# Input projection: the products with the high part of a weight tile all ahead of those with its low part

## The chip, the cores and the metric

The program runs on one core of one Trainium2 chip. The metric is device time in microseconds (us) from the start of one execution to its end; lower is better. Each time shown here is a median of several executions, or the span of one execution that the hardware profiler recorded.

## The reference, cut to what matters

One layer of a hybrid decoder is computed for 256 prompt tokens and 8 x 4 sample tokens, 288 token rows in all:

```python
def hybrid_layer(x, ...):
    proj = x @ p['w_in']                  # (288 x 2048) @ (2048 x 5968): the input projection
    y_r, s_T, new_shift = rwkv_time_mix(proj[..., :RWKV_COLS], ...)     # 16 heads x 64, a recurrence
    y_n, ... = nsa_mix(proj[..., RWKV_COLS:], ...)    # compressed, selected and window attention
    h = jnp.concatenate([y_r, y_n], axis=-1) @ p['w_out']
    x = layer_norm(DEEPNORM_ALPHA * x + h, ...)
    f = peer_ffn(x, ...)                  # product-key experts: scores, top 16, gathered rows
    return layer_norm(DEEPNORM_ALPHA * x + f, ...)
```

The change touches the first line alone, and there only the order in which its partial products are summed.

## The kernel before

**The input projection.** The function `product` (L404) computes one block of up to 128 projected columns for all 288 tokens. The 2048 rows of the weight are taken as 16 chunks of 128, four to a weight tile, so a block has four weight tiles. A tile arrives by one or two transfers into `wraw` (4 buffers, L412). ScalarE casts it to the rounded high part `wh` (L415), and VectorE, or GpSimd for the last tile of a block, subtracts to get the low part `wl` (L417); `wh` and `wl` have 3 buffers each. The tokens are split in the same way, once, into `XH` and `XL`. TensorE then accumulates three products for each chunk in one of two PSUM banks `pj` (L422): `wh` by `XH`, `wh` by `XL`, `wl` by `XH`. That is 12 matmuls for a tile, 48 for a block, and 2256 for the 47 blocks of the kernel. The block is read out by `shift_mix` (L755, for the recurrence) or by a copy on ScalarE (L493, L507, for the attention).

**What else runs in that stage.** While the projection runs, GpSimd gathers pages of the compressed cache (`co`, 4 buffers, issued at L453 behind the last `wl` that GpSimd made), VectorE adds them up with weights (`CA`, L474 and L476), and VectorE, ScalarE and GpSimd do the elementwise work of the recurrence for each pair of heads (`head_pair`, L757 to L824). Later the chunked recurrence itself (`prompt_steps`, lines from L1085 on) is woven into the projection of the attention columns.

**What sets the order.** The kernel is written as generators that `weave` interleaves in program order, and then a list scheduler in the framework orders each engine's instructions by when it believes their operands to be ready. Each engine executes its own list strictly in that order. So an edit to the order of matmuls can also change what stands ahead of what on the other engines, and on the DMA queue of SyncE (SP), which issues the weight transfers.

**After the projection** come the sample states and the attention over the caches, the output projection with its own loop (L1706), the query products of the experts (L1865), a dense product of all experts (L1911), and the weighted sum of the expert rows (L1957 to L2119). None of them calls `product`.

Of the kernel before, what the change touches and what calls it, by code (L numbers as in the profile page):

```python
# [2 lines left out]

# [1 line left out]

# [143 lines left out]
def hybrid_decode_step(ctx: ExitStack, tc: tile.TileContext, a, outs, dbg=None):  # L149
# [37 lines left out]
    def bank(tag="pb"):  # L187
        places = [(pool, nm, n) for _, div in psum for t_, pool, nm, n in div for _ in range(n) if t_ == tag]
        turn[tag] = k = (turn.get(tag, -1) + 1) % len(places)
        pool, nm, n = places[k]  # L190
        return pool.tile([P, 512], F32, name=tag, tag=nm, bufs=n)
# [169 lines left out]
    for q in range(8):  # L361
        pb = bank(("p0", "p1")[q % 2])
        for t in range(2):
            for e in range(2):
                k = 2 * q + e
# [38 lines left out]
    def product(pool, pieces, xh, xl, zero=None, n=P, lo=None, m=8, nt=NT):  # L404

        pb = bank("pj")
        for o in range(0, 16, m):
            w = pool([P, m, P], "wraw", bufs=WB)
            if zero is not None:
                ve.memset(w[:, :, zero[0]:zero[1]], 0.0)  # L410
            for src, c0, c1 in pieces:
                last[0] = sy.dma_start(w[:, :, c0:c1], src.rearrange("(k p) c -> p k c", p=P)[:, o:o + m])  # L412
            wh = pool([P, m, P], "wh", F32R, bufs=WH)
            wl = pool([P, m, P], "wl", F32R, bufs=WH)
            sc.copy(wh[:, :, :n], w[:, :, :n])  # L415
            en = lo or (gp if o // m in LOG else ve)
            i_ = en.tensor_tensor(wl[:, :, :n], w[:, :, :n], wh[:, :, :n].bitcast(F32), OP.subtract)  # L417
            if en is gp:
                last[1] = i_
            for k in range(m):  # L420
                for wi, xi in ((wh, xh), (wh, xl), (wl, xh)):
                    last[2] = pe.matmul(pb[:n, :nt], wi[:, k, :n], xi[(o + k) // 8][:, (o + k) % 8, :nt],  # L422
                                        start=(o + k == 0 and wi is wh and xi is xh), stop=(o + k == 15 and wi is wl))
        return pb

    w_in = a["w_in"][0]
    def proj(*cols, **kw):
        o, pieces = 0, []
        for c0, c1, *at in cols:
            o = at[0] if at else o  # L430
            pieces.append((w_in[:, c0:c1], o, o + c1 - c0))
            o += c1 - c0
        return product(wp, pieces, *([x_[:, :8], x_[:, 8:]] for x_ in (XH0, XL0)), m=WM, **kw)
# [1332 lines left out]
    for t in range(2):  # L1766
        for q in range(4):
# [5 lines left out]
            for e in range(4):  # L1773
                k = 4 * q + e
# [430 lines left out]
```

## Time and profile before

| what | us |
|---|---|
| median of 3 executions | 2430.81 |
| lowest and highest of them | 2426.59, 2439.01 |
| the profiled execution, its own time | 2431.03 |
| its span in the trace | 2429.3 |
| first and last start of a matmul of the input projection (L422) | 20.1, 516.6 |
| busy time of those 2256 matmuls, by product: wh XH, wh XL, wl XH | 231.6, 227.7, 232.8 |
| TensorE idle just ahead of them, by product | 13.8, 0.0, 11.4 |
| casts to wh on ScalarE (188), mean of one | 0.616 |
| subtractions to wl on VectorE (141), mean of one | 0.716 |
| subtractions to wl on GpSimd (47), median of one | 1.293 |

The page gives the granted clock of TensorE as a share of full speed, a mean of 0.954 over the span. An instruction's idle time is that of its engine just before it, and the arrow names what ended it. Matmuls are pipelined: one shows as 0.29 us long, and the next starts 0.13 us after it.

### The profile page before, as it was taken

The page shows a single profiled execution, that of the slowest core. Times are in us where ns is not written, and L with a number is a line of the kernel's source. Part 1 is how long each engine was busy: PE and PEld are TensorE (multiplying, and loading weights), DVE is VectorE, ACT ScalarE, POOL GpSimd, SP SyncE. Part 2 cuts the span into 40 slices and gives each one's busy share as a digit, 9 for nine tenths or more (in the row PEclk, how much of TensorE's full clock was granted, in tenths as well). Part 3 has the DMA queues.
Part 4 walks back from the last instruction along what each step waited for, and adds up shares of the span by engine and source line. Part 5 has one row for each costly group of instructions (what it writes and reads, how often), then busy time and mean ns, then how long its engine had stood idle before and what let it go on. Part 6 is the DMA issues. An engine that isn't in the chain of part 4 may idle for free.

```text
span 2429.3 us, 42430 instructions
## 1 busy us (share of the span) xinstructions
PE 2241.3 (92%) x15564; PEld 1877.2 (77%) x15564; DVE 1755.8 (72%) x4053; ACT 824.8 (34%) x1609; POOL 1292.9 (53%) x1342
## 2 busy tenths in 40 slices
PE   7989999896897898889999999998998999999996
PEld 7978898894644566678888888887777888887885
DVE  5789766555374345789867777566777899998888
ACT  4433222223333343220111111112776444443443
POOL 5678423223264211648755556464442688876772
PEclk9989999998698898899999999998999999999998
DMA  7777985447468974989899999997664899999994
GB/s 219 233 227 237 277 226 166 128 135 240 159 232 257 330 261 160 347 303 382 306 376 372 373 388 385 357 405 273 188 193 122 312 359 361 359 361 356 349 361 178
DMA packets 311025, 683.42 MB, mean 281 GB/s; under 512 B 82239, under 2 KB 184577, under 8 KB 309889
## 3 DMA queue, kind: packets, MB, share of 16 engines
q1 hardware_dynamic: 229600, 341.93, 41.9%
q0 software_dynamic: 81216, 338.78, 38.9%
q8 instruction: 123, 2.02, 0.3%
q14 instruction: 86, 0.70, 0.1%
HBM read 665.04 MB, written 23.88 MB: 284 GB/s over the span
## 4 chain that ended last, share of the span: by engine, by line
PE 69%; DMA 8%; DVE 7%; issue 6%; POOL 5%; ACT 3%; SPq 1%; POOLq 0%; DVEq 0%; ACTq 0%
PE pb L2119 18%; PE ph L1911 15%; PE pj L422 7%; PE pj L1865 5%; PE pa L1706 3%; PE px L1957 3%; PE pa L1990 2%; DMA co<-in_cache_cmp_kv,gidx 2%; POOL rows L453 2%; DMA rows<-in_peer_u_g,gi 2%; PE p L1096 2%; PE pt L1949 2%; PE fs L2009 1%; PE sa L923 1%; PE ss L1535 1%
## 5 line engine op out<-in xcount | busy, mean ns | idle before, releaser
L1911 PE MATMUL ph<-Xfd,ur 128*128 128x256 f32 x2304 | 497.6, 379 | 0.0
L1911 PEld LDWEIGHTS ph<-Xfd,ur 128*128 128x128 f32 x2304 | 437.6, 190 | 59.4
L453 POOL DMA_INDIRECT rq<-in_peer_v_g,gi x256 | 380.6, 1487 | 150.4 <-DVE fP L2092 85.6
L453 POOL DMA_INDIRECT rows<-in_peer_u_g,gi x256 | 297.3, 1161 | 204.6 <-DVE rows L1835 117.1
L1835 DVE SCALAR_TENSOR_TENSOR rows<-rows,x1a 128x896 f32<-128x896 f32 x256 | 280.9, 1104 | 136.2 <-DMA rows<-in_peer_u_g,gi 133.6
L422 PE MATMUL pj<-XH,wh 128*128 128x288 f32 (+1 forms) x752 | 231.6, 308 | 13.8 <-DVE ss L755 6.0
L422 PE MATMUL pj<-XH,wl 128*128 128x288 f32 (+1 forms) x752 | 232.8, 310 | 11.4 <-POOL wl L417 5.8
L422 PE MATMUL pj<-XL,wh 128*128 128x288 f32 (+1 forms) x752 | 227.7, 303 | 0.0
L2092 DVE SCALAR_TENSOR_TENSOR fP<-rq,ge,fP 128x640 f32<-128x640 f32 x254 | 223.6, 880 | 2.5
L2119 PE MATMUL pb<-vl,ah 128*128 128x512 f32 (+1 forms) x768 | 207.1, 378 | 0.8
L2119 PE MATMUL pb<-vh,al 128*128 128x512 f32 (+1 forms) x768 | 205.4, 375 | 0.0
L2119 PE MATMUL pb<-vh,ah 128*128 128x512 f32 (+1 forms) x768 | 186.7, 378 | 13.4 <-ACT vh L2111 10.9
L1912 ACT COPY AW<-ph 128x256 f32<-128x256 f32 x128 | 76.5, 614 | 360.4 <-PE ph L1911 321.0
L415 ACT CAST wh<-wraw 128x512 fp32r<-128x512 f32 (+1 forms) x188 | 114.7, 616 | 228.9 <-PE pj L422 178.8
L2119 PEld LDWEIGHTS pb<-vh,ah 128*128 128x128 f32 x768 | 144.8, 195 | 35.7 <-ACT vh L2111 13.9
L476 DVE SCALAR_TENSOR_TENSOR CA<-co,wbc,CA 128x256 f32<-128x256 f32 x248 | 129.8, 561 | 46.7 <-DMA co<-in_cache_cmp_kv,gidx 46.6
L2119 PEld LDWEIGHTS pb<-vl,ah 128*128 128x128 f32 x768 | 145.0, 195 | 23.0 <-DVE vl L2112 3.8
L422 PEld LDWEIGHTS pj<-XH,wl 128*128 128x128 f32 (+1 forms) x752 | 145.5, 194 | 21.6 <-DVE wl L417 8.0
L422 PEld LDWEIGHTS pj<-XH,wh 128*128 128x128 f32 (+1 forms) x752 | 146.0, 194 | 20.1 <-DVE ss L755 6.4
L2119 PEld LDWEIGHTS pb<-vh,al 128*128 128x128 f32 x768 | 145.0, 194 | 19.4
L422 PEld LDWEIGHTS pj<-XL,wh 128*128 128x128 f32 (+1 forms) x752 | 146.0, 194 | 1.5 <-issue 1.2
L417 DVE TENSOR_TENSOR wl<-wraw,wh 128x512 fp32r<-128x512 f32 (+1 forms) x141 | 99.9, 716 | 41.2 <-ACT wh L415 38.3
(869 smaller groups left out, 4281.1 us busy)
## 6 DMA issues: line engine op xcount, KB each, us to landing
ur<-in_peer_u_t SPq DMA_DIRECT2D x128, 576.0 KB
wraw<-in_w_in SPq DMA_DIRECT2D x152, 256.0 KB
cw<-in_w_out SPq DMA_DIRECT2D x32, 512.0 KB
wraw<-in_w_out SPq DMA_DIRECT2D x32, 512.0 KB
wraw<-in_peer_wq SPq DMA_DIRECT2D x32, 512.0 KB
cw<-in_peer_wq SPq DMA_DIRECT2D x32, 512.0 KB
wraw<-in_w_in SPq DMA_DIRECT2D x64, 128.0 KB
co<-in_state_win_kv SPq DMA_DIRECT2D x16, 512.0 KB
```

Source lines behind the costliest of these rows:

```text
L415: sc.copy(wh[:, :, :n], w[:, :, :n])
L417: i_ = en.tensor_tensor(wl[:, :, :n], w[:, :, :n], wh[:, :, :n].bitcast(F32), OP.subtract)
L422: last[2] = pe.matmul(pb[:n, :nt], wi[:, k, :n], xi[(o + k) // 8][:, (o + k) % 8, :nt], start=(o + k == 0 and wi is wh and xi is xh), stop ...
L453: gp.indirect_dma_start(out=dst, out_offset=None, in_=rows_, in_offset=bass.IndirectOffsetOnAxis(ap=ix, axis=0))
L476: ve.scalar_tensor_tensor(d_, x_, w_, d_, op0=OP.mult, op1=OP.add)
L1706: pe.matmul(acc[t], xi[:, e, P * t:P * t + P], wi[:, e, :], start=(k == e == n_ == 0), stop=(k == 6 and e == 1 and n_ == 2))
L1835: i_ = ve.scalar_tensor_tensor(r_, r_, 1.0, X1a[t], op0=OP.mult, op1=OP.mult, accum_out=h_)
L1865: pe.matmul(pq[c][:, :NPR], w[:, k, 128 * c:128 * c + 128], XT[:, 4 * g + k, :], start=(g == k == 0), stop=(g == k == 3))
L1911: mm = pe.matmul(ph[:, :NPR], w[:, e, :], Xfd[:, e, :], start=(e == 0), stop=(e == NDB - 1))
L1912: return mm, sc.copy(AW[:, i1 // 64, :, i1 % 64], ph[:, :NPR])
L2092: ve.scalar_tensor_tensor(fP[t], r_, w_, fP[t], op0=OP.mult, op1=OP.add)
L2119: pe.matmul(acc[3 * t + q][:, :n_], wi[:, P * t:P * t + P], xi[:, 512 * q:512 * q + n_], start=(k == 0 and wi is ah and xi is vh), stop=(k ...
```

## The change

The three products of a chunk were issued chunk by chunk. Now a weight tile's eight products with `wh` are issued first, chunk by chunk, and then its four products with `wl`. The flags that start and end the accumulation stay with the first and the last matmul of the block. Nothing else is edited.

```diff
+import itertools
...
-            for k in range(m):
-                for wi, xi in ((wh, xh), (wh, xl), (wl, xh)):
+            for pairs in (((wh, xh), (wh, xl)), ((wl, xh),)):
+                for k, (wi, xi) in itertools.product(range(m), pairs):
                     last[2] = pe.matmul(pb[:n, :nt], wi[:, k, :n], xi[(o + k) // 8][:, (o + k) % 8, :nt],
                                         start=(o + k == 0 and wi is wh and xi is xh), stop=(o + k == 15 and wi is wl))
```

Two lines are added above, so a line of the changed kernel has a number that is higher by 2.

**TensorE.** Here is the border between the first two weight tiles of the first block (tile 306/307, then 326/327; 96 columns wide), before:

```order
L422 MATMUL pj_301<-XL_131,wh_306 96x288
L422 MATMUL pj_301<-XH_130,wl_307 96x288
L422 MATMUL pj_301<-XH_130,wh_326 96x288
L422 MATMUL pj_301<-XL_131,wh_326 96x288
L422 MATMUL pj_301<-XH_130,wl_327 96x288
```

and now:

```order
L424 MATMUL pj_301<-XL_131,wh_306 96x288
L424 MATMUL pj_301<-XH_130,wl_307 96x288 x4
L424 MATMUL pj_301<-XH_130,wh_326 96x288
L424 MATMUL pj_301<-XL_131,wh_326 96x288
L424 MATMUL pj_301<-XH_130,wh_326 96x288
```

The first matmul that reads `wl` was the third of its tile and is now the ninth; the last that reads `wh` was the eleventh and is now the eighth.

**VectorE.** The next place is in the work for the fifth pair of heads. `ss_2598<-pj_2512` (L755) is the last part of the readout of a block from its PSUM bank, `wl_2809` the low part of the first weight tile of a later block, `CA` the adds of gathered pages, the other rows the recurrence's elementwise work. Before:

```order
L821 TENSOR_TENSOR ss_2598<-kx_2644,Di_2636 128x32
L755 SCALAR_TENSOR_TENSOR ss_2598<-pj_2512,ommu_181,Tmu_2600 128x32
L476 SCALAR_TENSOR_TENSOR CA_1633<-co_2671,wbc_91,CA_1633 128x256 x2
L821 TENSOR_TENSOR st_2597<-ta_2620,Di_2636 128x128 x2
L821 TENSOR_TENSOR ss_2598<-ta_2620,Di_2636 128x32
L476 SCALAR_TENSOR_TENSOR CA_1633<-co_2671,wbc_91,CA_1633 128x256 x2
L809 TENSOR_TENSOR BV_95<-pb_2650,st_2597 128x128 x2
L809 TENSOR_TENSOR BV_95<-pb_2650,ss_2598 128x32
L476 SCALAR_TENSOR_TENSOR CA_1633<-co_2700,wbc_91,CA_1633 128x256 x2
L782 SCALAR_TENSOR_TENSOR L_2920<-CT1_100,tw_2912 128x256
L476 SCALAR_TENSOR_TENSOR CA_1633<-co_2700,wbc_91,CA_1633 128x256 x2
L417 TENSOR_TENSOR wl_2809<-wraw_2806,wh_2808 128x512
```

and now:

```order
L757 SCALAR_TENSOR_TENSOR st_2597<-pj_2512,ommu_181,Tmu_2600 128x128 x2
L818 TENSOR_TENSOR st_2597<-rx_2585,De_2633 128x2x64 x2
L803 SCALAR_TENSOR_TENSOR kk_2643<-K8_278,PT_63,pb_2641 128x288
L478 SCALAR_TENSOR_TENSOR CA_1633<-co_2671,wbc_91,CA_1633 128x256
L478 SCALAR_TENSOR_TENSOR CA_1633<-co_2700,wbc_91,CA_1633 128x256
L757 SCALAR_TENSOR_TENSOR ss_2598<-pj_2512,ommu_181,Tmu_2600 128x32
L820 TENSOR_TENSOR ss_2598<-rx_2585,ss_2598 128x32
L817 TENSOR_TENSOR st_2597<-kk_2643,De_2633 128x2x64 x2
L478 SCALAR_TENSOR_TENSOR CA_1633<-co_2700,wbc_91,CA_1633 128x256
L804 TENSOR_TENSOR kx_2644<-K8_278,fk_2624 128x288
L819 TENSOR_TENSOR ss_2598<-kk_2643,ss_2598 128x32
L419 TENSOR_TENSOR wl_2809<-wraw_2806,wh_2808 128x512
```

Behind the readout, `wl_2809` stood behind eight adds of pages and seven other instructions, and now stands behind one add and five others. In return two adds have come between the parts of the readout.

**The queue of SP**, at the start of the output projection. `cw` and `wraw` are tiles of weights of 512 KB each, for the sample tokens and for the prompt tokens. Before:

```order
L1568 DMA SKT<-in_subkeys_t 128x2048
L1695 DMA wraw<-in_w_out 128x2x512 x2
L1533 DMA cw<-in_w_out 128x1024
L1695 DMA wraw<-in_w_out 128x2x512
L1533 DMA cw<-in_w_out 128x1024 x2
```

and now:

```order
L1570 DMA SKT<-in_subkeys_t 128x2048
L1697 DMA wraw<-in_w_out 128x2x512 x3
L1535 DMA cw<-in_w_out 128x1024 x2
L1747 DMA wraw<-in_peer_wq 128x4x256 x2
L1535 DMA cw<-in_w_out 128x1024
```

The third tile of the prompt tokens has moved ahead of one tile of the sample tokens. From the dense product of the experts (L1911) on, the orders of TensorE and of SP are unchanged, while on the other engines a few instructions of the expert selection near its start changed places.

## The prediction

> **What bounds the kernel now.** I read the page's busy shares first, then its costliest groups.
>
> ```profile
> PE 2241.3 (92%) x15564; PEld 1877.2 (77%) x15564; DVE 1755.8 (72%) x4053; ACT 824.8 (34%) x1609; POOL 1292.9 (53%) x1342
> ...
> L422 PE MATMUL pj<-XH,wh 128*128 128x288 f32 (+1 forms) x752 | 231.6, 308 | 13.8 <-DVE ss L755 6.0
> L422 PE MATMUL pj<-XH,wl 128*128 128x288 f32 (+1 forms) x752 | 232.8, 310 | 11.4 <-POOL wl L417 5.8
> ```
>
> TensorE is busy 92% of the span, so only its idle time can come back. The edit touches one stage. There, TensorE is idle 13.8 us ahead of a product `wh` by `XH`, and 11.4 us ahead of a product `wl` by `XH`. The 11.4 us is what the edit aims at and is 0.47% of the span, so even all of it would hardly be seen. The view by stretches gives the stage and some parts of it. Its columns are length, busy time of PE, PEld, DVE, ACT and POOL with counts, clock, DMA share and GB/s:
>
> ```profile
> 20.00:517.00 497.00, 465.82 (x4981) 425.65 (x4980) 351.00 (x746) 162.18 (x338) 255.39 (x395) 0.96 0.71 206
> 130.00:153.00 23.00, 17.03 (x106) 14.55 (x105) 22.84 (x58) 7.56 (x17) 18.20 (x31) 0.87 0.79 235
> 165.00:174.00 9.00, 6.64 (x41) 5.62 (x42) 9.00 (x21) 2.88 (x8) 6.13 (x12) 1.00 0.61 172
> 174.00:190.00 16.00, 15.34 (x89) 13.24 (x87) 15.12 (x38) 5.83 (x13) 14.94 (x28) 0.89 0.70 218
> 190.00:217.00 27.00, 24.07 (x168) 19.69 (x167) 25.28 (x67) 10.56 (x25) 21.79 (x43) 0.97 0.92 285
> ```
>
> Over the stage VectorE is busy 351 of 497 us, but not evenly: between 165 and 217 it works 9.00 + 15.12 + 25.28 = 49.4 of 52 us. An engine that has 2.6 us of rest there can be late for TensorE whatever order TensorE takes.
>
> **What the edit gives a `wl`.** The timeline of TensorE shows the pace (start, length, instruction). Between these two rows lie 12 steps:
>
> ```profile
> 25.74 0.29 PE L422 MATMUL pj<-XL,wh 128*128 128x288 f32 x1
> ...
> 27.33 0.29 PE L422 MATMUL pj<-XL,wh 128*128 128x288 f32 x1
> ```
>
> (27.33 − 25.74) / 12 = 0.133 us from one matmul to the next. The first `wl` matmul was third of its tile and becomes ninth, so six matmuls of work that needs no `wl` come ahead of it: 6 × 0.133 = **0.80 us of slack for each weight tile**. The last read of `wh` was eleventh and becomes eighth, so its buffer is freed 3 × 0.133 = 0.40 us sooner; the cast that refills it, and the `wl` behind that, can start by as much earlier. The last reads of `wl` and of the block are where they were, so `wraw`, `wl` and `pj` come free as before. There are as many matmuls, weight loads, casts and transfers as before, and no instruction or wait is added.
>
> **Where the 11.4 us are.** I looked at every idle time ahead of a `wl` matmul in the timeline. There are 13, each behind exactly two matmuls of its tile. These nine matter by name, with two other waits that follow them:
>
> ```profile
> 40.16 0.40 PE L422 MATMUL pj<-XH,wl 128*128 128x288 f32 x1 [0.56 <-POOL wl L417]
> ...
> 45.23 0.58 PE L422 MATMUL pj<-XH,wh 128*128 128x288 f32 x1 [3.48 <-DVE lo L755]
> ...
> 126.33 0.40 PE L422 MATMUL pj<-XH,wl 128*128 128x288 f32 x1 [2.03 <-POOL wl L417]
> ...
> 129.44 0.61 PE L422 MATMUL pj<-XH,wl 128*128 128x288 f32 x1 [0.17 <-DVE wl L417]
> ...
> 152.42 0.61 PE L422 MATMUL pj<-XH,wh 128*128 128x288 f32 x1 [5.97 <-DVE ss L755]
> ...
> 165.28 0.40 PE L422 MATMUL pj<-XH,wl 128*128 128x288 f32 x1 [0.76 <-DVE wl L417]
> ...
> 173.56 0.40 PE L422 MATMUL pj<-XH,wl 128*128 128x288 f32 x1 [1.48 <-DVE wl L417]
> ...
> 188.70 0.40 PE L422 MATMUL pj<-XH,wl 128*128 128x288 f32 x1 [0.66 <-DVE wl L417]
> ...
> 205.66 0.40 PE L422 MATMUL pj<-XH,wl 128*128 128x288 f32 x1 [0.72 <-DVE wl L417]
> ...
> 209.53 0.40 PE L422 MATMUL pj<-XH,wl 128*128 128x288 f32 x1 [0.82 <-POOL wl L417]
> ...
> 215.37 0.54 PE L422 MATMUL pj<-XH,wl 128*128 128x288 f32 x1 [1.40 <-DVE wl L417]
> ```
>
> Behind 217 four are left, shown here as a group over 217 to 517:
>
> ```profile
> L422 PE MATMUL pj<-XH,wl 128*128 128x288 f32 x398 | 122.5, 308 | 2.8 <-POOL wl L417 2.4 <-DVE wl L417 0.4
> ```
>
> ```profile
> 421.89 0.40 PE L422 MATMUL pj<-XH,wl 128*128 128x288 f32 x1 [1.65 <-POOL wl L417]
> ```
>
> With 0.80 us of slack each wait loses the smaller of itself and 0.80. Part by part:
>
> *Up to 153: nothing.* What is won at 40.16 is lost at 45.23, where the next block waits 3.48 us for a readout by VectorE. What is won at 126.33 and 129.44 (0.80 + 0.17) is lost at 152.42: TensorE waits 5.97 us there for a bank that VectorE reads out last, and VectorE was busy 22.84 of the 23 us before. Late next is VectorE, and it isn't sped up.
>
> *165 to 217: −4.0 us.* The six waits lose 0.76 + 0.80 + 0.66 + 0.72 + 0.80 + 0.80 = 4.54. The ends are wider. If VectorE sets the pace alone, the slack can be used once and all later waits stand: 0.80. If the new order on VectorE and the earlier casts take away whole waits: 0.76 + 1.48 + 0.66 + 0.72 + 0.82 + 1.40 = 5.84. That the last of them goes whole can be read from the order rows shown with the change. Between the readout and `wl_2809` there now stand one add and five other instructions, where fifteen stood. These are the readout, the `wl` and its cast before, and the groups by which I price the new queue:
>
> ```profile
> 208.22 0.24 DVE L755 SCALAR_TENSOR_TENSOR ss<-pj,ommu,Tmu 128x32 f32<-128x32 f32 x1
> ...
> 211.50 0.63 ACT L415 CAST wh<-wraw 128x512 fp32r<-128x512 f32 x1
> ...
> 214.63 0.68 DVE L417 TENSOR_TENSOR wl<-wraw,wh 128x512 fp32r<-128x512 f32 x1
> ```
>
> ```profile
> L476 DVE SCALAR_TENSOR_TENSOR CA<-co,wbc,CA 128x256 f32<-128x256 f32 x35 | 20.9, 624 | 2.6 <-DMA co<-in_cache_cmp_kv,gidx 2.6
> ...
> L802 DVE TENSOR_TENSOR kx<-K,fk 128x288 f32<-128x288 f32 x3 | 2.4, 803 | 1.3 <-POOL fk L779 1.3
> ...
> L815 DVE TENSOR_TENSOR st<-kk,De 128x128 f32<-128x128 f32 x6 | 1.5, 282 | 0.0
> ...
> L817 DVE TENSOR_TENSOR ss<-kk,ss 128x32 f32<-128x32 f32 x3 | 1.2, 414 | 0.0
> ...
> L818 DVE TENSOR_TENSOR ss<-rx,ss 128x32 f32<-128x32 f32 x3 | 0.5, 176 | 0.0
> ```
>
> From the readout's start to the start of `wl_2809` was 214.63 − 208.22 = 6.4 us. Now it is 0.24 + 0.18 + 2 × 0.28 + 0.62 + 0.80 + 0.41 = 2.8 us, by which it would be ready to start at 211.0. Its cast ends at 211.50 + 0.63 = 212.13, so it starts there, 2.5 us sooner, against a wait of 1.40. With two adds more inside the readout (2 × 0.62) it still starts by 212.3. Of 4.54 and these two ends I take 4.0, near the first: the row of 165 to 174 shows VectorE with no rest at all, so a part of the gain at 173.56 should come back as a later `wl`.
>
> *217 to 517: −1.0 us.* The four waits lose at most the group's 2.8; with 0.80 at 421.89, 2.8 − 0.85 = 1.9. VectorE has rest here, yet two of the waits are for GpSimd, which the new order serves no sooner. Between 0 and 1.9 I take the middle.
>
> **The clock: 0 us.** Three stretches of 3.4 us ran at a clock of 0.50 (the third number from the end). The rows show two of them with the stretch ahead of each:
>
> ```profile
> 123.30:126.70 3.40, 1.37 (x11) 1.14 (x9) 1.23 (x5) 0.93 (x2) 3.15 (x9) 1.00 0.97 334
> 126.70:130.10 3.40, 3.23 (x15) 2.89 (x14) 2.70 (x8) 0.98 (x3) 1.19 (x2) 0.50 0.76 239
> ...
> 212.10:215.50 3.40, 2.00 (x11) 1.00 (x8) 3.29 (x8) 1.48 (x4) 3.27 (x7) 1.00 1.04 361
> 215.50:218.90 3.40, 3.40 (x20) 3.12 (x22) 3.40 (x7) 1.58 (x4) 2.34 (x9) 0.50 0.57 160
> ```
>
> A stretch in which TensorE was busy 1.37 or 2.00 of 3.40 us (40 and 59%) was followed by one at half clock, which does 1.7 us of work in 3.4. Shorter waits can lift such a stretch over the border: 2.03 to 1.23 us of waiting makes 1.37 into 2.17 (64%). With the like case near 174, up to 3 × 1.7 = 5.1 us could come back. But where the border lies no row says, and a shift of some us can also put a fresh stretch on an idle piece; I take 0, between −5.1 and a loss that the slow rival prices.
>
> [...]
>
> **The output projection: 0 us.** On SP's queue the third prompt tile passes one tile of the sample tokens, one transfer of 512 KB. This stage moved 283 GB/s:
>
> ```profile
> 774.00:1050.00 276.00, 229.11 (x1438) 156.86 (x1436) 157.16 (x456) 91.89 (x231) 86.61 (x102) 0.87 0.81 283
> ```
>
> So one tile is 524,288 / 283,000 = 1.85 us earlier and the other as much later. One of the two loops may wait for it: −1.85 to +1.85, and 0 as the bytes are the same. The stages behind it keep TensorE's order and SP's, and so their times.
>
> **The sum.** −4.0 − 1.0 = −5.0 on the profiled execution's own 2431.03 gives **2426.0**. That execution lies 0.2 above the median shown, 2430.81, so no correction is made. The forecast's own ends: 2431.0 − 5.84 − 2.8 − 5.1 − 1.85 = 2415, and 2431.0 − 0.8 + 1.85 = 2432.
>
> **The rivals.** *Nothing comes back (2431, chance 0.16).* The waits ahead of `wl` go, but VectorE or GpSimd is late elsewhere: TensorE waits as long ahead of `wh` or for a readout. For it: VectorE's 49.4 of 52 us, and the two places above where I already count this. Against it: the `wl` of 215.37 moves ahead of adds of pages, for which TensorE isn't waiting in any row there.
>
> *Everything comes through (2418, chance 0.13).* No absorption: the thirteen lose 0.56 + 0.97 + 4.54 + 1.9 = 8.0, and the three half-clock stretches go, 5.1: 2431.0 − 13.1 = 2418. For it: the stretches lie right behind these waits. Against it: the 5.97 us at 152.42.
>
> *The readout gets late (2442, chance 0.11).* The new order puts adds of gathered pages ahead of or into readouts of a `pj` bank: five more at the fifth pair of heads and two more at each of two later pairs, 9 × 0.62 = 5.6 us. An add may also wait for its gather, and then the readout behind it does too; one such wait was up to 3.9 us:
>
> ```profile
> DVE CA L476 <- DMA co<-in_cache_cmp_kv,gidx: 40.9, 24, 3.9
> ```
>
> With one half-clock stretch, 1.7, this is 5.6 + 3.9 + 1.7 = 11.2: 2442. It decides from the point where the readout ends later than the other bank's block lasts, 48 × 0.133 = 6.4 us; short of that TensorE doesn't notice. The wait at 152.42 is of this kind, so the point can be reached. *The change doesn't do what it says:* the order rows exclude this, as the `wl` matmuls stand ninth to twelfth.
>
> **How the numbers follow.** The forecast has 0.60. No rival reaches far, so the range is the forecast's, less 2.5 below and 8 above: the executions before lay from 2426.6 to 2439.0 about 2430.8. That is 2413 to 2440; outside are the slow rival's 0.11 and some outlying part of the rest. A measurement of this kernel tells about 0.5%, 12.2 us, from no change. Faster by more, below 2418.7: half of the 2418 case and the lower tail of the forecast, 0.07 + 0.11 = 0.18. Slower by more, above 2443: most of the slow rival, 0.10. The rest, 0.72, is within.
>
> **What would show it.** In the changed profile, idle time ahead of the `wl` products should fall from 11.4 to about 4 us, what is left being waits of at most 1.3. If the 13.8 us ahead of `wh` by `XH` grow by as much, the first rival holds. The last projection matmul should start about 5 us sooner than 516.6, and the stages behind should be as long as before. Adds before a readout followed by a wait ahead of a `wh` matmul, longer than before, would show the slow rival; a clock of 1.00 in the stretches behind 126, 174 and 215 the fast one. Wrong steps to look for first: the 4.0 between 165 and 217, and the clock's 0.

## The result and the profile after

Over 18 runs each, the changed kernel takes 2447.14 us (median; 2433.74 to 2460.52) and the one before 2429.77 us (2416.92 to 2439.01). The ratio is 1.0074, with a 95% interval of 1.0057 to 1.0091. That is **18 us slower** and lies outside the range of the prediction. The profiled execution took 2453.46 us with a span of 2451.7, that is 22.4 us more than the span of before. So the differences between the stages of the two traces add up to some 4 us more than the 18.

Here are the page's busy shares and then, from the view of groups by line (count, busy time, mean ns, idle time ahead with its releasers), what changed in the input projection:

```profile
PE 2232.3 (91%) x15564; PEld 1869.4 (76%) x15564; DVE 1751.1 (71%) x4053; ACT 825.2 (34%) x1609; POOL 1313.7 (54%) x1342
```

```profile
L424 PE MATMUL pj<-XH,wh 128*128 128x288 f32 (+1 forms) x752 | 215.6, 308 | 21.0 <-DVE ss L757 8.2 <-ACT wh L417 7.0 <-DVE lo L757 4.9
L424 PE MATMUL pj<-XL,wh 128*128 128x288 f32 (+1 forms) x752 | 212.1, 302 | 0.0
L424 PE MATMUL pj<-XH,wl 128*128 128x288 f32 (+1 forms) x752 | 137.6, 304 | 5.6 <-DVE wl L419 5.1 <-issue 0.5
L1098 PE MATMUL p<-T,SB 64*64 64x64 f32 x640 | 25.3, 226 | 5.6 <-DVE SC L1090 4.1 <-DVE T L1133 1.5
L1098 PE MATMUL p<-TT,W 64*64 64x64 f32 x640 | 24.8, 226 | 6.0 <-DVE W L1120 6.0
```

The same groups of the recurrence before:

```profile
L1096 PE MATMUL p<-T,SB 64*64 64x64 f32 x640 | 25.3, 222 | 0.4 <-issue 0.4
L1096 PE MATMUL p<-TT,W 64*64 64x64 f32 x640 | 24.9, 222 | 2.3 <-DVE W L1118 2.3
```

The waits ahead of `wl` did what the edit is for: 11.4 us became 5.6. (Their busy time of 137.6 us is no gain: one takes 304 ns on average, 310 before, but four of them now follow each other and overlap, and a group's busy time counts an overlap once: 752 × 304 ns would be 228.6 us.) Yet 7 us more stand ahead of `wh`, and 9 more ahead of two groups of the recurrence, which the edit doesn't name.

The view by stretches, cut at the last projection matmul and at the first and last product of the output projection (L1706, now L1708), is first of before and then of after. Its columns are length, busy time of PE, PEld, DVE, ACT and POOL with counts, granted clock, DMA share and GB/s:

```profile
517.00:790.00 273.00, 225.21 (x2405) 148.33 (x2404) 147.53 (x493) 91.98 (x227) 113.11 (x157) 0.87 0.68 216
790.00:1037.00 247.00, 218.00 (x1373) 150.62 (x1372) 136.34 (x399) 85.02 (x214) 72.18 (x76) 0.90 0.79 274
```

```profile
20.00:526.30 506.30, 456.55 (x4971) 418.00 (x4971) 349.38 (x745) 162.51 (x338) 254.02 (x393) 0.97 0.70 202
526.30:798.00 271.70, 223.49 (x2411) 146.19 (x2411) 142.76 (x492) 92.06 (x227) 116.51 (x164) 0.88 0.68 218
798.00:1054.00 256.00, 219.87 (x1373) 151.65 (x1373) 142.89 (x403) 85.64 (x214) 75.56 (x71) 0.89 0.78 266
```

The projection ends 9.4 us later (526.3 against 516.9), and the output projection, of which the edit changes no line, takes 256 us where it took 247. A further 5.7 us lie between the dense product and the first picks of the experts (12.5 us idle against 6.8). So in these two traces more than half of the loss stands behind the stage that was edited.

### The profile page after: what moved, and what is told of

Same layout as the page of the kernel before. It is cut to its first block, busy times and chain, and to the rows that moved or that the text cites. A ratio compares the mean times of both kernels' runs of the same rounds, so it can differ in the third digit from the quotient of the medians.

```text
span 2451.7 us, 42421 instructions
## 1 busy us (share of the span) xinstructions
PE 2232.3 (91%) x15564; PEld 1869.4 (76%) x15564; DVE 1751.1 (71%) x4053; ACT 825.2 (34%) x1609; POOL 1313.7 (54%) x1342
## 4 chain that ended last, share of the span: by engine, by line
PE 54%; DMA 17%; DVE 10%; issue 9%; POOL 7%; ACT 3%; SPq 0%; POOLq 0%; DVEq 0%; ACTq 0%
PE pb L2121 18%; DMA rows<-in_peer_u_g,gi 8%; PE pj L424 6%; PE pj L1867 5%; POOL rows L455 4%; DMA co<-in_cache_cmp_kv,gidx 3%; PE pa L1708 3%; PE px L1959 3%; PE pa L1992 2%; PE p L1098 2%; DVE rows L1837 2%; PE pt L1951 2%; PE sa L925 1%; DVE CA L478 1%; PE fs L2011 1%
## 5 line engine op out<-in xcount | busy, mean ns | idle before, releaser
L455 POOL DMA_INDIRECT rows<-in_peer_u_g,gi x256 | 312.0, 1219 | 194.5 <-DVE rows L1837 115.2
L424 PE MATMUL pj<-XH,wh 128*128 128x288 f32 (+1 forms) x752 | 215.6, 308 | 21.0 <-DVE ss L757 8.2
L424 PE MATMUL pj<-XL,wh 128*128 128x288 f32 (+1 forms) x752 | 212.1, 302 | 0.0
L2121 PE MATMUL pb<-vh,ah 128*128 128x512 f32 (+1 forms) x768 | 186.7, 378 | 13.4 <-ACT vh L2113 13.4
L424 PE MATMUL pj<-XH,wl 128*128 128x288 f32 (+1 forms) x752 | 137.6, 304 | 5.6 <-DVE wl L419 5.1
L424 PEld LDWEIGHTS pj<-XH,wl 128*128 128x128 f32 (+1 forms) x752 | 112.5, 191 | 13.7 <-DVE wl L419 7.1
## 6 DMA issues: line engine op xcount, KB each, us to landing
wraw<-in_w_in SPq DMA_DIRECT2D x152, 256.0 KB
```

Source lines behind the costliest of these rows:

```text
L455: gp.indirect_dma_start(out=dst, out_offset=None, in_=rows_, in_offset=bass.IndirectOffsetOnAxis(ap=ix, axis=0))
L2121: pe.matmul(acc[3 * t + q][:, :n_], wi[:, P * t:P * t + P], xi[:, 512 * q:512 * q + n_], start=(k == 0 and wi is ah and xi is vh), stop=(k ...
```

## The experiments

**How they are made.** The edit changes two things: the order of twelve matmuls, and, through the scheduler, each engine's list. Compared place by place, 1298 of VectorE's 3215 instructions stand elsewhere in the changed kernel's list, more than half of them behind the projection; on SP it is 137 of 860. To part the two, a kernel is held to lists that a table names, by edges that order instructions of one engine and add no instruction and no semaphore:

```diff
+def keep_order(nc, tc):
+    traced = {i.name: i for i in nc.cur_bb.bb.instructions}
+    dep = mybir.DependencyInfo(mybir.DependencyClass.NoSync, mybir.DependencyReason.DATA)
+    for steps in json.loads(zlib.decompress(base64.b85decode(_ORDER))).values():
+        n, prev = 0, None
+        for step in steps:
+            n += step
+            i = traced.get(f"I-{n}")
+            if i is not None:
+                if prev is not None:
+                    tc.add_manual_dep(i, prev, dep, reason="order")
+                prev = i.name
...
         hybrid_decode_step(tc, a, outs)
+        keep_order(nc, tc)
```

Neither kernel was run held to its own lists; but e1 below, held to before's lists, takes before's time, so the holding itself costs nothing that can be seen. A list can be cut wherever both versions have executed the same set of instructions, so lists of before and of the changed kernel can be joined piece by piece. The pieces: P1, blocks 1 to 26 of the input projection; P2, its blocks 27 to 47; O1, the sample tokens' attention and the start of the output projection; O2, the rest of it; S, all behind. "New" means as in the changed kernel. Each ratio is to runs of before that were made beside it; their median lay between 2419.81 and 2434.42 us. The last column is the time from the first to the last product of the output projection in the run's one trace.

| run | products | new lists | ratio to before (95%) | output projection, us |
|---|---|---|---|---|
| e1 | new | none | 1.0001 (0.9974 to 1.0028) | 248.8 |
| e2 | old | all | 1.0106 (1.0065 to 1.0147) | 261.9 |
| e3 | new | P1 P2 | 1.0028 (1.0003 to 1.0053) | 245.5 |
| e4 | new | O1 O2 S | 1.0057 (1.0026 to 1.0088) | 258.9 |
| e5 | new | O1 O2 | 1.0044 (1.0015 to 1.0073) | 257.9 |
| e6 | new | S | 1.0010 (0.9985 to 1.0035) | 243.9 |
| e7 | new | SP's queue in O2 and a part of O1 | 0.9988 (0.9960 to 1.0017) | 249.6 |
| e9 | new | P1 | 1.0013 (0.9987 to 1.0038) | 245.9 |
| e10 | new | P2 | 0.9988 (0.9962 to 1.0014) | 247.0 |
| e15 | new | O2 | 0.9986 (0.9969 to 1.0004) | 251.5 |
| e16 | new | O1 | 1.0034 (1.0011 to 1.0058) | 255.9 |
| e17 | new | O1 O2, without SP's | 1.0045 (1.0024 to 1.0066) | 274.6 |
| e18 | new | P2 O2 | 1.0002 (0.9977 to 1.0028) | 251.2 |

### The products or the lists: e1 and e2

The edit of e1 is the change with the table of before's lists; that of e2 is the table of the changed kernel's lists alone.

> The new order of the products within each weight tile, but every engine's list is held to the places of before: only the twelve matmuls of a tile change places among themselves. Theory A (the loss comes from the lists that the scheduler dealt anew, the edit itself saves a little): 0 to 8 us faster than before, ratio 0.997 to 1.000. Theory B (the new order of the products costs by itself, by the wl buffers that are now read in one burst at a tile's end): as slow as the changed kernel, ratio near 1.007, and idle time ahead of the wh products of some 20 us as in the changed kernel (13.8 before).

> The old order of the products within each weight tile, with every engine's list held to the places of the changed kernel. Theory A: as slow as the changed kernel or slower, by up to the slack that it lacks: 17 to 26 us over before, ratio 1.007 to 1.011. Theory B: the time of before, ratio within 0.002 of 1.

Theory A holds: the products alone change nothing that can be measured, and the lists alone, with the products in their old order, cost 1.06%. The changed kernel, with the same lists and the new products, lies 0.32% below e2, as if the edit saved something there; but the two intervals overlap. The groups of e1 and of e2 show both halves:

```profile
L424 PE MATMUL pj<-XH,wh 128*128 128x288 f32 (+1 forms) x752 | 219.3, 312 | 16.9 <-DVE ss L757 6.7 <-ACT wh L417 5.3 <-DVE lo L757 3.8
...
L424 PE MATMUL pj<-XH,wl 128*128 128x288 f32 (+1 forms) x752 | 137.0, 302 | 6.6 <-DVE wl L419 5.1 <-POOL wl L419 1.3
L1098 PE MATMUL p<-T,SB 64*64 64x64 f32 x640 | 25.0, 221 | 0.4 <-DVE ss L819 0.4
```

```profile
L422 PE MATMUL pj<-XH,wl 128*128 128x288 f32 (+1 forms) x752 | 232.2, 309 | 13.7 <-DVE wl L417 10.9 <-POOL wl L417 2.6
...
L1096 PE MATMUL p<-T,SB 64*64 64x64 f32 x640 | 25.1, 224 | 5.2 <-DVE SC L1088 3.6 <-DVE T L1131 1.6
```

With the new products on the old lists (e1) the waits for `wl` nearly halve, from 11.4 to 6.6 us, and `T,SB` of the recurrence waits 0.4 us as before. With the old products on the new lists (e2) the waits for `wl` stay, and `T,SB` waits 5.2.

### By stage: e3 to e6

> The changed kernel, its lists kept up to the end of the input projection on each engine, and held to those of before from there on. By the two traces the projection ends 9.4 us later in the changed kernel and the output projection takes 7.6 us more. Theory A1 (both losses are real and add up): 8 to 11 us over before, ratio 1.0035 to 1.0045, and the stage after the projection as long as before. Theory A2 (what is lost in the projection is hidden or made up later): within 3 us of before.

> The counterpart: new order of the products, the lists of before up to the end of the input projection, those of the changed kernel from there on. Theory A1: the projection ends 0 to 8 us sooner than before, the output projection takes some 8 us more, sum 0 to 9 us over before, ratio 1.000 to 1.004. If the 5.7 us that the changed kernel's profiled execution lost between the dense product and the picks come from the lists too, 5 us more: up to 1.006.

> New order of the products; every engine's list as before, but from the end of the input projection to the end of the output projection as in the changed kernel. In three profiled executions with the new lists the output projection took 256 to 262 us from its first to its last matmul, in three with the old ones 246 to 249. If that is the loss: 8 to 14 us over before, ratio 1.003 to 1.006. If the loss behind the projection arises in the expert selection: within 3 us of before.

> New order of the products; every engine's list as before, but from the end of the output projection on as in the changed kernel. TensorE stood idle 12.2 to 13.5 us between the dense product and the first picks with the new lists, 5.4 to 8.7 with the old ones. If this comes from the lists behind the output projection: 4 to 8 us over before, ratio 1.0015 to 1.003, and that gap 12 us or more. If it is only a late end of what went before: ratio within 0.001 and the gap 9 us or less.

The lists cost 0.28% in the projection (6.8 us of 2420, with an interval that begins at 0.7), 0.44% in O1 and O2 (10.7 us), and 0.10% in S, which can't be told from nothing. The three add up to 0.82%, with 0.74% for the changed kernel, and the two pieces behind the projection to 0.54%, with 0.57% for e4. In e6 the gap ahead of the picks was 12.7 us, as with the first theory; but runs with old lists there show up to 11.9 (e17), so the 5.7 us of the changed kernel's trace are not shown to come from the lists.

The stretch of the output projection in e5, against that of e1 with the old lists (first of e1):

```profile
768.40:1017.20 248.80, 216.33 (x1373) 149.57 (x1373) 136.49 (x399) 84.99 (x214) 72.20 (x75) 0.92 0.78 272
```

```profile
781.80:1039.70 257.90, 221.94 (x1373) 153.58 (x1373) 139.24 (x399) 85.63 (x214) 73.08 (x69) 0.88 0.77 265
```

The same 1373 matmuls take 9 us longer; 5.6 of them are busy time, at a granted clock of 0.88 instead of 0.92, and 3.5 are idle.

### Which list of the output projection: e7, e13 to e17

> New order of the products; every engine's list as before, but on SP's queue the transfers of the output projection stand as in the changed kernel (57 places, the swaps of weight tiles for prompt and sample tokens, and the first tiles of the query products moved ahead). If SP's queue makes the loss of the output projection: its waits for cw transfers rise from some 2 to 7 us, and the time by 6 to 12 us, ratio 1.0025 to 1.005. If, as the prediction had it, the swaps are worth at most 1.85 us: ratio within 0.002 of 1, and the loss is made by the lists of TensorE, VectorE and ScalarE.

SP's queue alone costs nothing that can be seen; its interval ends at 1.0017, 4 us. Next I looked at the longest piece of TensorE's list without a product of the prompt: 196 matmuls with the old lists, 250 with the new ones, 53.5 us in the trace of e1 and 69.6 in that of e5. To make it shorter, the sample tokens' chain was given a higher priority, which leaves the lists ahead of O2 as they were:

```diff
-    weave((take(chain, 36), 36), (prompt_attention(), 19, 300), (out_first(), 17))
+    weave((take(chain, 36), 36, 100), (prompt_attention(), 19, 300), (out_first(), 17))
```

e13 is the kernel before with this line; e14 is the change, held to e13's lists.

> The kernel before with one number more: the sample tokens' chain gets a higher priority in the output projection, so that the scheduler keeps more of the prompt's products (L1706) to lay among the chain's small steps. The lists differ from those of before only from the middle of the output projection on. The stretch of matmuls without a product of the prompt (196 in the list of before, 250 in that of the changed kernel) shrinks to 166. In the traces it lasted 53.5 us with 196 and 69.6 us with 250, that is 0.3 us for each matmul more, with 0.1 us of idle time and 0.19 us of half clock. If the length of this stretch decides what the output projection takes: a stretch of 44 to 46 us, the output projection 6 to 9 us shorter than the 247 us of before, ratio 0.9965 to 0.998. If the stretch only moves work about: the output projection within 2 us of 247, ratio within 0.001 of 1.

> The new order of the products within each weight tile, every engine's list held to that of the run with the sample tokens' chain first. As the products alone changed the time by 0.01% (0.9974 to 1.0028), the same as that run: if the stretch decides, 6 to 9 us faster than before, ratio 0.9965 to 0.998; idle time ahead of wl products 3 to 7 us where it is 11 to 12 in the kernel before, and ahead of the recurrence 6 to 11 where it is 5. If the products are worth their 5 us after all: 11 to 14 us faster, ratio 0.994 to 0.9955.

This theory fell. e13 has a ratio of 1.0015 (0.9984 to 1.0045) and e14 of 1.0011 (0.9990 to 1.0033), where 0.998 or less was expected. The stretch shrank to 49 us in both, but the output projection took 247.2 and 253.4 us. So I cut the lists in two and took SP's queue out:

> New order of the products; every engine's list as before, but as in the changed kernel from the point at which SP's, TensorE's and ScalarE's lists begin to differ by long pieces (TensorE's place 5383, in the middle of the output projection's first half) to the end of the output projection. The stretch without a product of the prompt has 250 matmuls of the list, as in the changed kernel. If these pieces bring the 11 us: output projection 255 to 262 us from its first to its last matmul, 7 to 13 us over before, ratio 1.003 to 1.0055. If not: 244 to 251 us, ratio within 0.002 of 1.

> The counterpart: as in the changed kernel from the end of the input projection to that point, as before from there on; the stretch has 196 matmuls, as before. If the loss comes in the sample tokens' attention and the start of the output projection: 7 to 13 us over before, ratio 1.003 to 1.0055, and 275 us or more from the end of the input projection to the first matmul of the output projection (254 to 274 with the old lists). If it comes behind that point: within 0.002 of 1 and an output projection of 244 to 251 us.

> As the run with the new lists in the output projection, but SP's queue as before. In that run TensorE waited some 5 us longer for cw transfers than with the old lists. If SP's queue shares in the loss only together with TensorE's new list: output projection 250 to 254 us, 4 to 7 us over before, ratio 1.0015 to 1.003. If the queue has no share: 256 to 262 us, ratio 1.003 to 1.006.

The long stretch is in O2, and O2 costs no time that can be seen (0.9986), though its one trace has an output projection of 251.5 us. O1 costs 0.34%, 8.2 us (2.7 to 14.0), and with SP's queue as before the loss is the same (1.0045 against 1.0044). Half of what was expected of e16 came: not the attention became longer (267 us, as in other runs), but the output projection (255.9 us). Here are the stretches between the 33rd and the 65th prompt product, first of e15 with the old list of O1, then of e16:

```profile
790.30:841.50 51.20, 44.18 (x362) 27.38 (x361) 20.71 (x88) 18.10 (x65) 4.53 (x6) 0.93 0.97 335
```

```profile
791.20:856.50 65.30, 55.49 (x393) 33.96 (x392) 24.84 (x113) 20.12 (x75) 2.87 (x2) 0.82 0.82 286
```

These two don't hold the same work: the lists put the 33rd and the 65th product at different places, and 362 matmuls lie between them in e15, 393 in e16. With one kernel's lists throughout it is 385 with the old ones (first, e1) and 370 with the new ones (the changed kernel):

```profile
779.90:835.50 55.60, 47.09 (x385) 29.12 (x384) 25.15 (x113) 19.93 (x75) 4.63 (x6) 0.94 0.91 323
```

```profile
808.10:866.60 58.50, 49.37 (x370) 29.78 (x369) 20.58 (x88) 18.37 (x66) 3.41 (x4) 0.88 0.89 315
```

In the six traces with the new list of O1 (the changed kernel, e2, e4, e5, e16, e17) this piece takes 55.9 to 70.0 us (mean 61.1), in twelve with the old one (all others but e8 and e11) 49.6 to 55.6 (mean 53.3), so some 8 us more. (e8, with lists near the old ones, has 56.6.) In four of the six there is a second run at half clock, of 6.8 to 27.3 us, which no trace with the old list has. The new list also has TensorE wait 2.2 us for a small product's operand in every trace (`sa` for VectorE's `Sc`).

A seventh trace speaks against so simple a reading. From the end of the input projection to the end of the output projection e11 (below) has the changed kernel's lists, but for nine places on TensorE and four on VectorE. Its piece takes 53.4 us, with the same wait of 2.2 us but no second run at half clock, and its output projection 248.5 us. Without that second run the piece takes 53.4 to 56.1 us (e2, e5, e11), hardly more than with the old list; with it, 58.5 to 70.0. The whole output projection has 50.3 to 114.1 us at half clock in the seven traces (mean 69.7) and 39.9 to 57.0 in the twelve (mean 48.2); e17 is far above the rest with its 114.1. Half of the difference, 10.8 us (an estimate from the granted 0.50), is about what the seven are longer, 10.9 us (259.1 against 248.2). So the loss of this stage goes with time at half clock. That the short waits of the new list bring the half clock on is argued, not shown, and e11 had the wait without it.

### Which part of the projection: e9 and e10

> New order of the products; every engine's list as in the changed kernel for the first 26 blocks of the input projection, as before from there on. In the traces with new lists TensorE stood idle 5 us longer ahead of wh products in blocks 1 to 20 and some 4 us longer in blocks 21 to 26 (with wh, wl and recurrence taken together) than with the old ones. If the late readouts of the prediction's slow rival carry the projection's loss: 5 to 9 us over before, ratio 1.002 to 1.0035, and 15 us or more of idle time ahead of wh products in the first 20 blocks. If the waits of the recurrence carry it: within 3 us of before.

> The counterpart: lists as before for 26 blocks, as in the changed kernel from there to the end of the input projection, then as before. With new lists TensorE stood idle 12 to 17 us ahead of the recurrence's matmuls there, with old ones 4 to 8 us, while its waits ahead of wh products fell by 3. If the recurrence's waits carry the projection's loss: 4 to 8 us over before, ratio 1.0015 to 1.0035. If the readouts carry it: within 3 us of before.

The times settle nothing: 1.0013 and 0.9988, against 1.0028 for both pieces, with intervals that overlap. The two add up to 1.0001, so the projection's 0.28% rests on the time of e3 alone. The traces lean to P1: from the first product to the start of the 27th block it took 244.4 to 248.0 us in three traces with the new list of P1 and new products (the changed kernel, e3, e9), and 233.6 to 242.9 in eleven with the old list (e1, e4 to e7, e10, e14 to e18). The waits ahead of `wh` in these 26 blocks were 18.4 to 20.1 us in the three, 11.1 to 14.2 in the eleven. For P2, TensorE did stand idle 13.4 us ahead of the recurrence in e10, yet P2 lasted 257.7 us there and 256.0 in e18, against 249.6 to 256.9 in nine traces with the old lists of the whole projection: most of the waits of the recurrence took the place of others. By the times, where in the projection the 6.8 us arise stays open.

### Other deals: e8 and e11

Nothing is held in these two. e8 groups the products by two chunks, and e11 takes the new order in GpSimd's tile alone:

```diff
-            for pairs in (((wh, xh), (wh, xl)), ((wl, xh),)):
-                for k, (wi, xi) in itertools.product(range(m), pairs):
+            for h, pairs in itertools.product(range(0, m, 2), (((wh, xh), (wh, xl)), ((wl, xh),))):
+                for k, (wi, xi) in itertools.product(range(h, h + 2), pairs):
```

```diff
-            for pairs in (((wh, xh), (wh, xl)), ((wl, xh),)):
+            two = ((((wh, xh), (wh, xl)), ((wl, xh),)) if en is gp else (((wh, xh), (wh, xl), (wl, xh)),))
+            for pairs in two:
```

> Nothing is held; the products are grouped by two chunks in place of four (four products with wh, two with wl, and again), so the first wl product is the fifth of its tile and the slack is 2 matmuls, 0.27 us. The scheduler deals lists that lie nearer to those of before: of VectorE's 3215 places 450 differ, against 1298 in the changed kernel, of SP's 860 places 35, against 137. If the lists decide: within 6 us of before, ratio 0.9975 to 1.0025. If the loss grows with the distance between wh and wl products: about a third to a half of the changed kernel's, 6 to 9 us, ratio 1.0025 to 1.004.

> Nothing is held; only the last weight tile of each block, whose low part GpSimd makes, takes its products in the new order, the other three tiles keep the old one. From the middle of the output projection on the scheduler deals the same lists as for the changed kernel; in the projection they differ from both. If the lists decide: the output projection takes 256 to 262 us from its first to its last matmul, and the time is 8 to 18 us over before, ratio 1.003 to 1.0075. If the loss grows with the number of tiles in the new order: a quarter of the changed kernel's, 4 to 5 us, ratio 1.0015 to 1.002, and an output projection of 250 us or less.

e8, with lists near those of before, has 1.0005 (0.9979 to 1.0030): no loss, as the lists would have it, though its interval doesn't quite shut out a third of the changed kernel's. e11, with a quarter of the edit and lists far from those of before, has 1.0038 (1.0010 to 1.0065), 9 us, which lies in the range for the lists and is twice what a quarter of the loss would be. In its trace the output projection took 248.5 us and not 256. That execution took 2436.83 us, 5.7 less than the median of its runs, so the trace doesn't show where the others lost their time.

### Before once more, and the best pieces: e12 and e18

> The kernel before, unchanged, for a second trace of it. If the traces of one kernel agree in the waits by kind: 11 to 14 us idle ahead of wl products, 12 to 16 ahead of wh products, 4 to 10 ahead of the recurrence, and an output projection of 244 to 250 us. If the profiled execution of before was an odd one, its 4.6 us ahead of the recurrence and 11.4 us ahead of wl will not come again.

The second trace of before has 11.8 us ahead of `wl`, 16.2 ahead of `wh`, 5.2 ahead of the recurrence, and an output projection of 247.0 us; 11.4, 13.8, 4.6 and 247.2 were the first. The waits by kind can be compared between traces to some 2 us.

> New order of the products, and the two pieces of the new lists that alone gave 0.9988 and 0.9986: those of the input projection from block 27 on, and those of the second half of the output projection; all else as before. If the pieces add up and the edit's saving with them: ratio 0.996 to 0.9985, 4 to 10 us faster than before. If both ratios were chance about the 1.0001 of the products alone: 0.999 to 1.001.

e18 stands at 1.0002 (0.9977 to 1.0028), as it would if the 0.9988 and 0.9986 were chance; of the gain that was expected if they add up (0.996 to 0.9985) its interval holds only the smaller end. No version that was run is shown to be faster than the kernel before.

## Why the prediction was wrong

**The slack of 0.80 us for each tile: right.** Waits ahead of `wl` fell to 5.6 us (about 4 was forecast), and to 2.1 to 7.1 in the nine traces with new products and the old lists of the projection (e1, e4 to e7, e14 to e17).

**−4.0 between 165 and 217, −1.0 behind: not borne out by the traces, and not settled by the time.** In e1 alone it looks as forecast: from the start of the block at 152 to that of the block at 213 it gained 2.0 us on before, and 2.6 more to the end of the stage. But on the mean of the nine these two parts take 60.0 and 301.2 us, and with the same lists and the old products (before, e12, e13) 60.0 and 301.4. The projection ended at 509.3 to 520.1 (mean 513.9), against 511.8 to 517.5 (mean 515.4), and nearly all of this 1.5 us lies ahead of 152, where nothing was forecast. What came ahead of `wl` went elsewhere: mean waits ahead of `wl`, `wh` and the recurrence are 4.8, 16.8 and 8.0 us, sum 29.6, against 12.0, 14.6 and 4.6, sum 31.2. That is the first rival, nothing comes back, and e1's 1.0001 fits it. Its interval also holds the −5.0 that I forecast.

**The failing step: lists dealt anew were priced in two places, and at nothing elsewhere.** The prediction had "**The output projection: 0 us.**", from SP's queue alone, with ±1.85, and "The stages behind it keep TensorE's order and SP's, and so their times." The first term asked the wrong queue: SP's new order is indeed worth nothing that can be seen (e7: 0.9988), but TensorE's, VectorE's and ScalarE's lists in that stage are new as well, and they cost 10.7 us (e5), with or without SP's (e17), of it 8.2 in O1 (e16). The second sentence leaves out VectorE: behind the output projection 509 of its instructions in the trace stand elsewhere, place by place, up to 1528 us, many more than the few that the text on the change speaks of. What that costs, e6 can't tell (0.10%, −0.15 to 0.35). For the projection, lists were priced in the sum only where they helped (`wl_2809`), and otherwise in a rival; they cost 6.8 us (e3, barely clear of nothing). The sum, by what the runs give, is 0 for the products, 6.8 for the projection's lists, 10.7 for the output projection's and 2.4 ± 6 for the rest: 19.9, where 18 was measured.

**The slow rival: its mechanism is in the traces, but only a part of the loss is its own.** It had adds of pages that wait for their gather ahead of a readout at the fifth pair of heads and two later ones. In the changed kernel VectorE indeed stood idle 4.00 us for a gather there. TensorE then waited 2.12 us for a `wl` that stood behind this add and, at the next block, 1.36 us for the readout:

```profile
210.38 0.48 DVE L478 SCALAR_TENSOR_TENSOR CA<-co,wbc,CA 128x256 f32<-128x256 f32 x1 [4.00 <-DMA co<-in_cache_cmp_kv,gidx]
...
214.92 0.24 DVE L757 SCALAR_TENSOR_TENSOR ss<-pj,ommu,Tmu 128x32 f32<-128x32 f32 x1
```

```profile
215.30 0.37 PE L424 MATMUL pj<-XH,wh 128*128 128x288 f32 x1 [1.36 <-DVE ss L757]
```

One pair earlier it is the same: two adds wait 2.2 to 3.9 us for a gather ahead of the readout in all four traces with the new list of P1 (the changed kernel, e2, e3, e9), and TensorE's next `wh` product is 2.6 to 3.3 us late in the three with new products, though a cast or an add is named as what ended that wait. That makes up a part of the 6 to 7 us more ahead of `wh` in P1; its share of the time isn't shown. The larger loss lies in the output projection, of which the rival says nothing, so that its 2442 came near the 2447 is in part luck.

VectorE's new list also reaches the recurrence. Here it is in the timeline of before and, below it, of after, at the recurrence's products `SC`:

```profile
232.06 0.47 DVE L476 SCALAR_TENSOR_TENSOR CA<-co,wbc,CA 128x256 f32<-128x256 f32 x1
232.45 0.68 DVE L1088 TENSOR_TENSOR SC<-p,CT 128x512 f32<-128x512 f32 x1
```

```profile
235.90 1.61 DVE L478 SCALAR_TENSOR_TENSOR CA<-co,wbc,CA 128x256 f32<-128x256 f32 x2
237.43 0.44 DVE L804 TENSOR_TENSOR kx<-K,fk 128x288 f32<-128x288 f32 x1
237.80 1.28 DVE L1090 TENSOR_TENSOR SC<-p,CT 128x512 f32<-128x512 f32 x2
```

```profile
238.63 1.15 PE L1098 MATMUL p<-T,SB 64*64 64x64 f32 x32 [2.44 <-DVE SC L1090]
```

Before, the second `SC` stood right behind one add; now both stand behind two adds and `kx`, and TensorE waits 2.44 us for them.

**The clock, 0 us: right for the products, not for the lists.** The prediction speaks of three stretches of 3.4 us; the trace of before has 37.5 us at half clock between 20 us and the end of the projection, the longest piece 10.2 us about the wait at 152.42. In e1 those three are gone, the sign named for the fast rival, and the time is still that of before. On the mean the nine traces have 28.8 us (20.5 to 41.0) and the three with old products 28.4 (20.5 to 37.5). That a border in TensorE's busy share decides was my assumption, and the trace of before shows none: a stretch of 3.4 us with TensorE busy 52% (420.26 to 423.68) was followed by a clock of 1.00, and one with 68% (300.80 to 304.21) by 0.50. In the output projection the clock did take part (0.88 against 0.92 in e5, and the 10.8 us above), where I gave it no term.

**The range** reached 8 us over the forecast's worst end, from the spread of before's runs, and left the slow rival outside with 0.11; the time lay 5 us above that rival.

## What to carry to other kernels

Where a scheduler deals the lists, an edit to one loop is two edits: hold the lists and measure each by itself. Here the loop was worth 0.01% (−0.26 to 0.28) and the lists 1.06% (0.65 to 1.47), and by e3 to e6 more than half of the lists' cost stood in a stage that the loop doesn't touch. In a forecast each stage whose lists are dealt anew, on any engine, needs a term with both signs of its own; a queue that comes out at zero doesn't speak for the others. A wait that is shortened can turn up as another wait: sum the waits by kind, not the one that the edit names. And where traces of one kernel differ by some us, compare all that share the lists in question: e1 by itself showed a gain that the mean of nine doesn't.

## What the runs showed of the hardware

One stage has two lengths with the same lists. The sample tokens' attention, from the end of the input projection to the first product of the output projection, took 273.1 us in the trace of before and 254.2 in e1, each with the lists of before; here are the stretches of e1, and of e7, which has those lists too:

```profile
514.50:768.40 253.90, 209.12 (x2405) 138.47 (x2405) 147.80 (x493) 91.89 (x227) 113.71 (x158) 0.92 0.73 233
```

```profile
520.10:792.00 271.90, 226.45 (x2405) 149.93 (x2404) 146.79 (x492) 92.24 (x227) 114.56 (x160) 0.85 0.68 218
```

By an estimate the clock makes most of the difference: 40 us at half clock in e1, 72 in before and 80 in e7, and half of 72 − 40 is 16 of the 19 us. (In the trace of before, a matmul of the input projection at a clock of 0.50 started 0.24 us after the one ahead of it, from 307.69 to 308.89, where it is 0.13 us at 1.00.) Three traces (e1, e3, e13) are of the short kind, 253.6 to 258.3 us, with old lists in this stage; the others lie between 263.9 and 277.1. So one trace can't show a gain or a loss of less than 20 us in this stage. The pieces at half clock are mostly 3.41 us long or a multiple of it: 24 of the 25 in the trace of before and 24 of the 25 in that of the changed kernel, where the last is 21.0 and 20.9 us. They start at other places in each, the first three at 44.80, 126.72 and 147.20 us in before and at 46.87, 152.68 and 193.64 in the changed kernel. The 19 us by which this one stage in the middle of the kernel moves are 0.8% of the whole.
